# First attention layer of a two-layer decoder: token sums kept in the weight sum's tile, head 1's products in another order, rope ahead of the weight splits, the last head's keys turned later

## The chip, the cores and the metric

The kernel runs on one core of a Trainium2 chip. The time is the device time of one execution in microseconds (us), the median of several runs. TensorE (PE) does the matrix products and the transposes, PEld is its load of weights, VectorE is DVE, ScalarE is ACT, GpSimd is POOL and SyncE is SP. SP and POOL start most of the transfers.

## The reference

Two residual layers over 512 tokens of width 2048, all in float32: `x <- x + W_out(mixer(RMSNorm(x)) * silu(gate))`. The first mixer, which the change touches, is differential attention in 8 heads. The second is RWKV-7. Of the first:

```
proj = h @ w_in                                  # 2048 -> 4 x 2048
q, k, v, gate = jnp.split(proj, 4, axis=-1)      # 8 heads; q and k twice 128 wide, v and gate 256 wide
q = apply_rope(rms_norm(q, q_gain), cos, sin)
k = apply_rope(rms_norm(k, k_gain), cos, sin)
a = softmax(q0 k0') - lam * softmax(q1 k1')      # causal, scale 128 ** -0.5
o = rms_norm(a @ v, subln_w) * (1.0 - lambda_init)
return (o * silu(gate)) @ w_out
```

## The kernel before, in words

Float32 products are made of two halves: a value is split into a high part (a cast on ACT) and the rest (a subtraction on DVE), and `mm3` (L116) adds three matmuls: high by high, high by low, low by high. A weight tile of 128 by 512 is split by L618 (`wh`, ACT) and L619 (`wl`, DVE), each with four buffers; tokens of the normalised input lie split in `hH` and `hL`, 16 tiles of 128 channels by 512 tokens.

The first layer, some 800 us of the span, goes head by head. For a head, the queries and keys (512 columns) and the values and gates (512 columns) are one product of 512 tokens x 2048 channels x 1024 columns.

- *Head 0* uses two plain products, `unit_tok`: queries and keys first, then values and gates (PE from about 55 to 105 us). Its four PSUM banks hold 128 tokens each.
- *Heads 1 to 7* use Strassen's scheme in Winograd's form (`Seven`, L532): seven products P1 to P7, each half as wide in tokens (256), channels (1024) and columns, so 48 matmuls of 512 columns each. P1 to P5 and P7 need sums of tokens or of weights, or both; only P2 and P3 take weights and tokens as they lie. `Seven.T` (8 tiles of 128 x 512) holds the running weight sum: `prime` (L606) loads it for head 1, POOL adds further blocks to it by accumulating transfers (`grow`, L591), `renew` loads it for the next head. Two pairs of PSUM banks, A and B, take turns; `copy` and `take` (L640 to L648) move and add them on ACT and DVE.
- *The token sums* S1, S2 and S4 (`S`, each split into halves) and the tokens' difference that replaces a half of `hH` and `hL` are made once, in four groups, during the second product of head 0: `forms` and `form_sums`, L550 to L583. A group needs two scratch tiles of 2 x 512 columns, which before lie in the tiles (tags) of V, VL and G.
- *After the products* of a head, `queries` (L650) applies rope (`rope`, L298: squares for the norm on ACT, four products with the tables on DVE) and the norm (`norm_qk`, L318: a chain of small DVE operations, then L328 scales the keys on ACT), and `turn_qk` (L357) transposes queries and keys, block by block of 128 tokens, on PE (L361) and splits them (L364 on ACT, L365 on DVE) into `qkT` and `qkL`. `VG.convert` (L376) scales the values (V, VL), and makes the gate G (a tanh on ACT, L381, and its product with the raw gate on DVE, L382).
- *Attention* of a head runs during the products of the next one, cut into steps by a `Chain` (L124): after so many matmuls (`tick`) it takes its next step. The turning of keys is such a chain too: in heads 1 to 6 one block every 9 matmuls, 32 matmuls or more after the last product has been written; in the last head every 4, and what is left is finished as soon as the last product ends. The last head's attention lies within the first of the products with `da_w_out` (the out-projection), whose rows are read back from DRAM (`yd`) by `Feed` (L483), 14 rows of 256 KB in a ring of 8, half of them in the tiles `t1`.

Instructions are put in order by a scheduler with priorities: what stands under `high_priority` with the greater offset goes first on its engine: SCAN (5000) for the chains' steps, AHEAD (2000) for the weights' loads and splits, 0 for the forms. Each engine then runs its own list in order, so that an instruction that waits holds all behind it.

Head 1 begins with P3, P2, and its T is loaded during head 0. The others begin with P7, P2. The order in which the products end matters: P5's end gives the keys and queries, P3's or P5's the last values and gates.

Of the kernel before, what the change touches and what calls it, by code (L numbers as in the profile page):

```python
# [13 lines left out]
F32 = mybir.dt.float32  # L14
# [3 lines left out]
AF = mybir.ActivationFunctionType  # L18
# [5 lines left out]
P = 128  # L24
D = 2048
T = 512
KT = D // P
NT = T // P
NH = 8
# [9 lines left out]
AHEAD, SCAN, SOLVE = 2000, 5000, 4000  # L39
# [41 lines left out]
class Halves:  # L81


    def __init__(self, parts, n):
        self.parts, self.n = parts, n
# [209 lines left out]
        self.rr = g.small.tile([P, NT, 4], F32, name="rr", tag="rr", bufs=2)  # L295


def rope(g, q, t):  # L298

    nc, t1 = g.nc, q.t1s[t]  # L300
    t2 = g.work.tile([P, 512], F32, name="t2", tag="p1", bufs=1)
    for c in range(4):
        cs = slice(c * P, (c + 1) * P)
        nc.scalar.activation(t2[:, cs], t1[:, cs], AF.Square, scale=g.rstd0[:, t : t + 1],
                             accum_out=q.ss[:, t, c : c + 1])
    t1v = t1[:].rearrange("p (a b c) -> p a b c", a=2, b=2)
    t2v = t2[:].rearrange("p (a b c) -> p a b c", a=2, b=2)

    def tab(x, lo, hi):
        return x[:, t, :, None, lo:hi].to_broadcast([P, 2, 2, hi - lo])  # L310

    nc.vector.tensor_mul(t2v[:, :, :, 0:64], t1v[:, :, :, 64:128], tab(g.S, 0, 64))
    nc.vector.tensor_mul(t2v[:, :, :, 64:128], t1v[:, :, :, 0:64], tab(g.S, 64, 128))
    nc.vector.tensor_mul(t1v, t1v, tab(g.C, 0, P))
    nc.vector.tensor_add(t1[:], t1[:], t2[:])


def norm_qk(g, q):  # L318

    nc, ss, rr = g.nc, q.ss, q.rr  # L320
    nc.vector.tensor_scalar(ss[:], ss[:], 1.0 / P, EPS, ALU.mult, ALU.add)
    rsqrt(g, rr[:].rearrange("p t c -> p (t c)"), ss[:].rearrange("p t c -> p (t c)"), 4 * NT, "r16")
    nc.vector.tensor_mul(rr[:], rr[:], g.rstd0[:, :, None].to_broadcast([P, NT, 4]))
    nc.vector.tensor_scalar(q.sq[:], rr[:, :, 0:2], P ** -0.5, None, ALU.mult)
    for t in range(NT):
        for c in (2, 3):
            cs = slice(c * P, (c + 1) * P)
            nc.scalar.activation(q.t1s[t][:, cs], q.t1s[t][:, cs], AF.Copy, scale=rr[:, t, c : c + 1])  # L328


def head_qk(g, qk):

    q = QK(g)
    for t in range(NT):
        with g.tc.high_priority(offset=AHEAD):
            g.nc.scalar.copy(q.t1s[t][:], qk[t][:])
    for t in range(NT):
        rope(g, q, t)
    norm_qk(g, q)
    return q  # L340


def head_qkT(g):

    w = g.work
    return (w.tile([P, 4, T], F32R, name="qkT", tag="qkT", bufs=1),
            w.tile([P, 4, T], F32R, name="qkL", tag="qkL", bufs=1))


def keys(g, q, qkT, gap):  # L350

    for t in range(NT):
        turn_qk(g, q.t1s, *qkT, t)
        yield gap
# [128 lines left out]
class Feed:  # L483

    def __init__(self, g, src, n, home):
        self.g, self.src, self.n, self.home, self.raw, self.rows = g, src, n, home, [], []
        self.load(6)
        self.split(4)  # L490

# [8 lines left out]

    def __call__(self, n, m):
        self.split(n + 1, m)
        self.load(n + 8)


class Tokens:
# [25 lines left out]
class Seven:  # L532
# [11 lines left out]

    def banks(self):
        g = self.g
        self.B, self.A = [[g.pp.tile([P, 512], F32, name="pp", tag="pp") for _ in range(2)] for _ in range(2)]
        self.U, self.W = [[g.const.tile([P, 512], F32, name="u", tag=f"dd{i}{x}") for x in "HL"] for i in range(2)]

    def forms(self, n, _):  # L550

        i = self.made
        if i == len(GROUPS) or n < 4 * i + 5:
            return
        self.made += 1
        if i == 0:
            self.prime(1)
        with self.g.tc.high_priority(offset=0):
            self.form_sums(i)

    def form_sums(self, i):

        g, k0 = self.g, GROUPS[i][0]
        nc = g.nc
        f = lambda ap: ap.bitcast(F32)
        tops, lows = [g.work.tile([P, 2, 512], F32, name="form", tag=("V", "VL", "G", "qkL")[(2 * i + x) % 3], bufs=1)
                      for x in range(2)]
        for o, kb in ((tops, k0), (lows, KP + k0)):
            for k in range(2):
                nc.vector.tensor_add(o[:, k], f(g.hH[kb + k][:]), f(g.hL[kb + k][:]))  # L570
        (a, b), (c, d) = [(x[:, :, 0:256], x[:, :, 256:512]) for x in (tops, lows)]
        s1, s2, s4 = [[self.S[nm][i][:, :, x, :] for x in range(2)] for nm in ("S1", "S2", "S4")]
        for dest, o, x, y, op in ((s1, d, b, d, ALU.subtract), (None, b, a, b, ALU.subtract),
                                  (s2, a, d, a, ALU.subtract), (s4, c, c, a, ALU.add)):
            nc.vector.tensor_tensor(out=o, in0=x, in1=y, op=op)
            if dest:
                nc.scalar.copy(dest[0], o)
                nc.vector.tensor_sub(dest[1], o, f(dest[0]))
# [68 lines left out]
            for o, a, b in zip(out, x, y):  # L647
                self.g.nc.vector.tensor_tensor(out=o[:], in0=a[:], in1=b[:], op=op)  # L648

    def queries(self, q, last):  # L650

        for t in range(NT):
            rope(self.g, q, t)
        norm_qk(self.g, q)
        qkT = head_qkT(self.g)
        turning = Chain(self.g, keys(self.g, q, qkT, 4 if last else 9), 1, self.g.ticks + 32)
        self.turning = None if last else turning
        return qkT

    def head(self, h):  # L660
# [39 lines left out]
        def scores():  # L700
            self.take(q01, q01, A if h == 1 else B)
            self.take(q23, A if h == 1 else B, W, sub)
            q.t1s = q01 + q23
            return self.queries(q, h == NH - 1)

        if h == 1:
            q01.extend(q.more(2))
            self.product(B, *P3)
            self.product(A, *P2)
            self.copy(U, B)  # L710
            self.product(B, *P7)
            self.copy(W, A)
            self.take(U, U, A)
            self.product(A, *P1)
            self.copy(q01, B)
            self.take(q01, q01, W, sub)
            self.product(B, *P4)
            self.take(W, W, A)
            self.product(A, *P6)
            self.take(q01, q01, B, sub)  # L720
            self.take(W, W, B)
            self.product(B, *P5)
            qkT = scores()
            late = (W, B)
        else:
            self.product(B, *P7)
            self.product(A, *P2, end=False)
            q01.extend(q.more(2))
            self.copy(q01, B)
            self.product(B, *P1)  # L730
            self.copy(U, A)
            self.product(A, *P4, first=False)
            self.copy(W, B)
            self.product(B, *P6)
            self.take(q01, q01, A, sub)
            self.take(W, W, A)
            self.product(A, *P5)
            qkT = scores()
            self.product(B, *P3)
            self.take(W, W, A)  # L740
            late = (U, B)
        for c in [c for c in g.chains if c is not self.turning]:
            c.finish(g)
        vg = VG(g)
        self.take(late[0], *late)
# [152 lines left out]
def layer0(g, aps):  # L898
# [87 lines left out]
    with ExitStack() as cx:  # L986
        g.work = cx.enter_context(tc.tile_pool(name="work", bufs=2))
        u = Seven(g, aps)
        q, qkT = head_qk(g, qk0), head_qkT(g)
# [942 lines left out]
```

## Time and profile before

| | us |
|---|---|
| median of 3 runs | 2085.8 (2085.49 to 2088.36) |
| profiled execution | 2084.43 |
| its span | 2082.7 |
| granted clock of PE over the span | 0.996 |
| PE busy | 2054.2 |
| DVE busy | 1679.5 |
| ACT busy | 1280.3 |

All rows are of that one profiled execution. A row of the timeline has the start in us from the span's beginning, the duration in us, engine, line, operation, names out<-in, shape, and in brackets the idle time of the engine before it with what ended it. PE's durations overlap, so that its pace is read from the distance of starts. Where a name like `t` or `wh` is seen, the scratch number is left out. A row of the windows has the window, its length, the busy time and number of instructions of each engine, then PE's granted clock as a share of full speed, the share of time in which the transfer engines were busy, and GB/s.

### The profile page before, as it was taken

To read this page: it belongs to the slowest core of one execution; us is meant where nothing else is said; L and a number is where in the kernel's file an instruction comes from. 1 tells how busy PE (TensorE), PEld (TensorE's weight loads), DVE (VectorE), ACT (ScalarE), POOL (GpSimd) and SP (SyncE) were. 2 spreads that over 40 slices of the span, in tenths; PEclk is the share of its full clock that TensorE was granted. 3 is DMA by queue.
4 is the path that set the end of the run, shared out by engine and by line. 5 is a ranking of instruction groups with operands and counts; after the bars stand their busy time and mean duration, and the time that the engine had idled before them with its cause. 6 is when DMAs were issued, how large, how long until landed. Compare 5 with 4: busy or idle time off the path is not lost. (4 is left out here: it accounts for less than half of the span.)

```text
span 2082.7 us, 35269 instructions
## 1 busy us (share of the span) xinstructions
PE 2054.2 (99%) x11924; PEld 1693.2 (81%) x11924; DVE 1679.5 (81%) x4379; ACT 1280.3 (61%) x3043; POOL 419.9 (20%) x733
## 2 busy tenths in 40 slices
PE   9989999999999999999999999999999999999999
PEld 8868788888888878888778888888888888877887
DVE  5978797888878886576878888888888888887745
ACT  6666676767667664356666666666666666665433
POOL 0011201102121100101233222232332223232001
PEclk9999999999999999999999999999999999999999
DMA  6467867879687666752212222222222222244665
GB/s 201 144 123 167 168 169 159 182 168 173 173 175 176 139 219 211 180 124 94 84 64 79 71 87 76 86 79 79 71 85 77 73 82 79 79 121 159 218 162 121
DMA packets 100774, 269.71 MB, mean 130 GB/s; under 512 B 12432, under 2 KB 28960, under 8 KB 100592
## 3 DMA queue, kind: packets, MB, share of 16 engines
q1 hardware_dynamic: 62016, 173.21, 26.0%
q0 software_dynamic: 24144, 78.23, 20.7%
q10 hardware_dynamic: 14432, 16.01, 2.3%
q8 instruction: 94, 1.54, 0.3%
q14 instruction: 88, 0.72, 0.1%
HBM read 251.41 MB, written 15.99 MB: 128 GB/s over the span
## 5 line engine op out<-in xcount | busy, mean ns | idle before, releaser
L118 PE MATMUL pp<-hH,wh 128*128 128x512 f32 x1024 | 416.7, 407 | 0.0
L118 PE MATMUL pp<-hL,wh 128*128 128x512 f32 x1024 | 411.9, 402 | 0.0
L118 PE MATMUL pp<-hH,wl 128*128 128x512 f32 x1024 | 411.6, 402 | 0.0
L109 ACT CAST wh<-wraw 128x512 fp32r<-128x512 f32 (+1 forms) x412 | 254.2, 618 | 215.2 <-PE pp L118 122.8
L110 DVE TENSOR_TENSOR wl<-wraw,wh 128x512 fp32r<-128x512 f32 (+1 forms) x412 | 292.3, 711 | 76.5 <-ACT wh L109 70.9
L118 PE MATMUL pp<-wh,hH 128*128 128x512 f32 x820 | 325.5, 397 | 9.9 <-DVE G L382 8.2
L118 PE MATMUL pp<-wl,hH 128*128 128x512 f32 x820 | 324.4, 396 | 0.0
L118 PE MATMUL pp<-wh,hL 128*128 128x512 f32 x820 | 324.0, 396 | 0.0
L118 PEld LDWEIGHTS pp<-hH,wh 128*128 128x128 f32 x1024 | 192.8, 188 | 38.0 <-issue 2.1
L118 PEld LDWEIGHTS pp<-hH,wl 128*128 128x128 f32 x1024 | 193.1, 189 | 33.3
L118 PEld LDWEIGHTS pp<-hL,wh 128*128 128x128 f32 x1024 | 193.1, 189 | 31.3
L118 PE MATMUL pp<-wh,S 128*128 128x512 f32 x672 | 211.3, 391 | 0.0
L118 PEld LDWEIGHTS pp<-wh,hH 128*128 128x128 f32 x820 | 155.0, 189 | 41.3 <-issue 8.6
L618 ACT CAST wh<-T 128x512 fp32r<-128x512 f32 x224 | 137.3, 620 | 71.5 <-PE pp L118 52.3
L118 PEld LDWEIGHTS pp<-wh,hL 128*128 128x128 f32 x820 | 155.2, 189 | 30.4
L118 PEld LDWEIGHTS pp<-wl,hH 128*128 128x128 f32 x820 | 155.3, 189 | 30.0 <-DVE wl L619 0.3
L1631 POOL COPY SA<-VS 64x64 f32<-64x64 f32 x224 | 75.4, 337 | 516.3 <-DVE VS L1649 463.0
L619 DVE TENSOR_TENSOR wl<-T,wh 128x512 fp32r<-128x512 f32 x224 | 152.3, 688 | 20.5 <-ACT wh L618 18.5
L591 POOL DMA_DIRECT2D T<-in_da_w_in_dram x84 | 72.3, 861 | 396.6 <-DMA wraw<-in_da_w_in_dram 195.4
L118 PEld LDWEIGHTS pp<-wh,S 128*128 128x128 f32 x672 | 125.9, 188 | 25.7
L1496 DVE SCALAR_TENSOR_TENSOR tmpl<-LT,n,Tm 128x60 f32<-128x60 f32 (+24 forms) x496 | 135.6, 273 | 13.4
L118 PE MATMUL pp<-wl,S 128*128 128x512 f32 x336 | 131.8, 392 | 0.0
(376 smaller groups left out, 4019.8 us busy)
## 6 DMA issues: line engine op xcount, KB each, us to landing
wraw<-in_rw_w_in_dram SPq DMA_DIRECT2D x128, 512.0 KB, 3.7
T<-in_da_w_in_dram POOLq DMA_DIRECT2D x84, 512.0 KB, 5.8
wraw<-in_da_w_in_dram SPq DMA_DIRECT2D x64, 512.0 KB, 4.2
T<-in_da_w_in_dram SPq DMA_DIRECT2D x28, 512.0 KB, 4.0
wraw<-in_da_w_out_dram SPq DMA_DIRECT2D x26, 512.0 KB, 4.2
wraw<-in_rw_w_out_dram SPq DMA_DIRECT2D x26, 512.0 KB, 4.2
wraw<-in_da_w_in_dram POOLq DMA_DIRECT2D x21, 512.0 KB, 6.5
yr<-yd SPq DMA_DIRECT2D x20, 256.0 KB, 2.8
```

Of the source, the lines that this page charges most:

```text
L109: nc.scalar.copy(hi[:], raw[:, k : k + n])
L110: g.split = nc.vector.tensor_sub(lo[:], raw[:, k : k + n], hi[:].bitcast(F32)).ins
L118: m = nc.tensor.matmul(out, a, b, start=s, stop=e, skip_group_check=skip)
L591: self.g.nc.gpsimd.dma_start(out=raw, in_=src, accum_op=ALU.add)
L618: g.nc.scalar.copy(hi[:], raw[:, k])
L619: g.nc.vector.tensor_sub(lo[:], raw[:, k], hi[:].bitcast(F32))
L1496: st = nc.vector.scalar_tensor_tensor(tt, LT[:, i : i + 1, i + 1 :].to_broadcast([P, s, n]), n2[:, i : i + 1], Tm[:, 0:s, i : i + 1].to_br ...
L1631: nc.gpsimd.tensor_copy(p.SA[r_, c - 1, :], VS[r_, c, h, :])
```

## The change

- `rope` writes the squares' unused result into the new `qkL` (`junk`) and no longer into `t2`. The tiles `qkT` and `qkL` are therefore taken before rope.
- The token forms use slots 0 to 3 and 4 to 7 of T in turn. So T can be loaded for head 1 only when the forms are done: `prime(1)` moves from the first form to head 1, after P2.
- Head 1's order P3 P2 P7 P1 P4 P6 P5 becomes P2 P7 P1 P4 P6 P5 P3, with P2 unsummed, alone in its banks; its sums are made accordingly. Now in every head P3 comes last, after the sums of queries and keys (`take` of q01 and q23) and `queries`.
- Rope and norm of heads 1 to 7 stand at AHEAD, the priority of the weight splits. The turning starts 34 matmuls after (32 before), with 9 in between in the last head too, where it is no longer finished at the end of the last product.
- Head 0's converts stand at AHEAD.
- The out-projection's rows lie in slots 0 to 3, 6 and 7 of T, a ring of 6; the last attention's steps are 20 matmuls apart (22).

```diff
-def rope(g, q, t):
+def rope(g, q, t, junk):
...
-        nc.scalar.activation(t2[:, cs], t1[:, cs], AF.Square, scale=g.rstd0[:, t : t + 1],
+        nc.scalar.activation(junk[:, c, t * P : (t + 1) * P], t1[:, cs], AF.Square, scale=g.rstd0[:, t : t + 1],
                              accum_out=q.ss[:, t, c : c + 1])
...
     def __call__(self, n, m):
         self.split(n + 1, m)
-        self.load(n + 8)
+        self.load(n + self.ring)
...
         self.made += 1
-        if i == 0:
-            self.prime(1)
         with self.g.tc.high_priority(offset=0):
             self.form_sums(i)
...
-        tops, lows = [g.work.tile([P, 2, 512], F32, name="form", tag=("V", "VL", "G", "qkL")[(2 * i + x) % 3], bufs=1)
-                      for x in range(2)]
+        tops, lows = [self.T[:, k : k + 2] for k in (i % 2 * 4, i % 2 * 4 + 2)]
...
-    def queries(self, q, last):
-
-        for t in range(NT):
-            rope(self.g, q, t)
-        norm_qk(self.g, q)
+    def queries(self, q):
+
         qkT = head_qkT(self.g)
-        turning = Chain(self.g, keys(self.g, q, qkT, 4 if last else 9), 1, self.g.ticks + 32)
-        self.turning = None if last else turning
+        with self.ahead:
+            for t in range(NT):
+                rope(self.g, q, t, qkT[1])
+            norm_qk(self.g, q)
+        self.turning = Chain(self.g, keys(self.g, q, qkT, 9), 1, self.g.ticks + 34)
         return qkT
...
         if h == 1:
+            self.product(A, *P2)
+            self.prime(1)
+            self.product(B, *P7)
+            self.copy(U, A)
+            self.product(A, *P1)
             q01.extend(q.more(2))
-            self.product(B, *P3)
-            self.product(A, *P2)
-            self.copy(U, B)
-            self.product(B, *P7)
-            self.copy(W, A)
-            self.take(U, U, A)
-            self.product(A, *P1)
...
-            self.product(B, *P5)
-            qkT = scores()
-            late = (W, B)
+            A, B = B, A
         else:
...
-            self.product(A, *P5)
-            qkT = scores()
-            self.product(B, *P3)
-            self.take(W, W, A)
-            late = (U, B)
+        self.product(A, *P5)
+        self.take(q01, q01, B)
+        self.take(q23, B, W, sub)
+        q.t1s = q01 + q23
+        qkT = self.queries(q)
+        self.product(B, *P3)
+        self.take(W, W, A)
...
         out = VG(g)
-        for t in range(NT):
-            out.convert(g, t, vg[t])
+        with tc.high_priority(offset=AHEAD):
+            for t in range(NT):
+                out.convert(g, t, vg[t])
...
-        feed = Feed(g, g.yd, KT - 2, lambda k: g.work.tile([P, T], F32, name="yr", tag="t1", bufs=4)[:] if k & 4 else
-                    Tt[:, k % 4])
+        feed = Feed(g, g.yd, KT - 2, lambda k: Tt[:, (0, 1, 2, 3, 6, 7)[k % 6]], 6)
...
-        ch = Chain(g, attention(g, NH - 1, *before, 22, rows, Tt[:, 4:6]), 12)
+        ch = Chain(g, attention(g, NH - 1, *before, 20, rows, Tt[:, 4:6]), 12)
```

What this does to the order of the instructions is seen at three places (line numbers of the changed kernel are 3 lower around L560 to L650 and 10 lower from L1000 on).

First, DVE at the end of head 0. Before (S_709 is the last group's S1, S_713 its S2, S_717 its S4, `form` their scratch):

```order
L575 TENSOR_TENSOR form<-form 128x2x256 x2
L578 TENSOR_TENSOR S_709<-form,S_709 128x2x256
L619 TENSOR_TENSOR wl<-wraw,wh 128x512 x2
L583 TENSOR_TENSOR hL<-form,hH 128x256 x2
L575 TENSOR_TENSOR form<-form 128x2x256 x2
L578 TENSOR_TENSOR S_713<-form,S_713 128x2x256
L578 TENSOR_TENSOR S_717<-form,S_717 128x2x256
L379 SCALAR_TENSOR_TENSOR VL<-pp,rstd_595,V 128x256 x3
L382 SCALAR_TENSOR_TENSOR G<-G,pp 128x256 x3
L379 SCALAR_TENSOR_TENSOR VL<-pp,rstd_595,V 128x256
L382 SCALAR_TENSOR_TENSOR G<-G,pp 128x256
```

And after, where the scratch is T:

```order
L365 TENSOR_TENSOR qkL<-pt,qkT 128x4x128
L379 SCALAR_TENSOR_TENSOR VL<-pp,rstd_595,V 128x256
L572 TENSOR_TENSOR T<-T 128x2x256
L379 SCALAR_TENSOR_TENSOR VL<-pp,rstd_595,V 128x256
L382 SCALAR_TENSOR_TENSOR G<-G,pp 128x256
L575 TENSOR_TENSOR S_709<-T,S_709 128x2x256
L382 SCALAR_TENSOR_TENSOR G<-G,pp 128x256
L379 SCALAR_TENSOR_TENSOR VL<-pp,rstd_595,V 128x256
L616 TENSOR_TENSOR wl<-wraw,wh 128x512
L379 SCALAR_TENSOR_TENSOR VL<-pp,rstd_595,V 128x256
```

The converts (VL, G) stood behind the whole last group; now they stand beside its first difference. The rest of the group, S2 and S4, has moved some forty rows down, behind the layer's small constants and between head 1's first weight splits of T and the attention's first masks (L403):

```order
L572 TENSOR_TENSOR T<-T 128x2x256
L616 TENSOR_TENSOR wl<-T,wh 128x512
L580 TENSOR_TENSOR hL<-T,hH 128x256 x2
L572 TENSOR_TENSOR T<-T 128x2x256
L616 TENSOR_TENSOR wl<-T,wh 128x512
L572 TENSOR_TENSOR T<-T 128x2x256
L403 ISA sc,mx<-sc,mask 128x128
L403 ISA mx 128x1
L616 TENSOR_TENSOR wl<-T,wh 128x512
L406 SCALAR_TENSOR_TENSOR nb<-mx,sq 128x1
L403 ISA sc,mx<-sc,mask 128x128
L403 ISA mx 128x1
```

Right behind these rows stand the differences `S_713<-T,S_713`, one L406 and `S_717<-T,S_717`, with which the second half of T is free.

Second, SP around the load of T for head 1. Before (t_1483 and t_1484 are P2's last two weight tiles):

```order
L76 DMA wraw<-in_da_w_in_dram 128x1024 x6
L593 DMA T<-in_da_w_in_dram 128x1024 x4
L76 DMA wraw<-in_da_w_in_dram 128x1024 x4
L593 DMA wraw<-in_da_w_in_dram 128x1024 x3
L593 DMA t_1483<-in_da_w_in_dram 128x512
L593 DMA t_1484<-in_da_w_in_dram 128x512
```

And after, where those two tiles are t_1327 and t_1328:

```order
L76 DMA wraw<-in_da_w_in_dram 128x1024 x10
L590 DMA wraw<-in_da_w_in_dram 128x1024 x2
L590 DMA t_1327<-in_da_w_in_dram 128x512
L590 DMA t_1328<-in_da_w_in_dram 128x512
L590 DMA wraw<-in_da_w_in_dram 128x1024
L590 DMA T<-in_da_w_in_dram 128x1024 x4
```

The four loads of T stood ahead of the last loads of head 0; now they stand behind P2's.

Third, PE at the last head's keys. Before, behind 48 matmuls of the out-projection's first unit (t_7477 and t_7478 are blocks of 128 tokens of queries and keys, `sc` the scores of the last head's attention):

```order
L118 MATMUL pp<-wh,hL 128x512
L361 MATMUL pt<-ident,t_7477 128x128 x2
L118 MATMUL sc<-qkT 128x128 x2
L361 MATMUL pt<-ident,t_7478 128x128 x4
L118 MATMUL sc<-qkL,qkT 128x128
```

And after, behind 8 of them (the same two blocks are t_7469 and t_7470):

```order
L118 MATMUL pp<-wl,hH 128x512
L361 MATMUL pt<-ident,t_7469 128x128 x2
L118 MATMUL pp<-wh,hL 128x512
L118 MATMUL pp<-wh,hH 128x512
L118 MATMUL pp<-wl,hH 128x512
L118 MATMUL pp<-wh,hL 128x512 x2
L118 MATMUL pp<-wh,hH 128x512
L361 MATMUL pt<-ident,t_7470 128x128 x4
```

The blocks followed each other with the scores between them; now products of the unit lie between them.

More of the change, by code (lines that the diff above doesn't have):

```diff
@@ L328, in norm_qk, with head_qk @@
             nc.scalar.activation(q.t1s[t][:, cs], q.t1s[t][:, cs], AF.Copy, scale=rr[:, t, c : c + 1])
-def head_qk(g, qk):
+def head_qk(g, qk, junk):
     q = QK(g)
@@ L337, in head_qk @@
     for t in range(NT):
-        rope(g, q, t)
+        rope(g, q, t, junk)
     norm_qk(g, q)
@@ L483, with __init__ @@
 class Feed:
-    def __init__(self, g, src, n, home):
-        self.g, self.src, self.n, self.home, self.raw, self.rows = g, src, n, home, [], []
+    def __init__(self, g, src, n, home, ring=8):
+        self.g, self.src, self.n, self.home, self.ring, self.raw, self.rows = g, src, n, home, ring, [], []
         self.load(6)
@@ L546, in banks @@
         g = self.g
-        self.B, self.A = [[g.pp.tile([P, 512], F32, name="pp", tag="pp") for _ in range(2)] for _ in range(2)]
+        self.A, self.B = [[g.pp.tile([P, 512], F32, name="pp", tag="pp") for _ in range(2)] for _ in range(2)]
         self.U, self.W = [[g.const.tile([P, 512], F32, name="u", tag=f"dd{i}{x}") for x in "HL"] for i in range(2)]
@@ L698, in head @@
         sub = ALU.subtract
[L700 to L704, printed above, removed]
-        if h == 1:
+        if h == 1:
+            self.product(A, *P2)
[3 more added lines that the diff above has]
+            self.product(A, *P1)
             q01.extend(q.more(2))
-            self.product(B, *P3)
-            self.product(A, *P2)
-            self.copy(U, B)
-            self.product(B, *P7)
+            self.copy(q01, B)
+            self.take(q01, q01, U, sub)
+            self.product(B, *P4)
             self.copy(W, A)
-            self.take(U, U, A)
-            self.product(A, *P1)
-            self.copy(q01, B)
-            self.take(q01, q01, W, sub)
-            self.product(B, *P4)
-            self.take(W, W, A)
+            self.take(W, W, U)
             self.product(A, *P6)
@@ L736, in head @@
             self.take(W, W, A)
-            self.product(A, *P5)
-            qkT = scores()
-            self.product(B, *P3)
-            self.take(W, W, A)
-            late = (U, B)
+        self.product(A, *P5)
[5 more added lines that the diff above has]
+        self.take(W, W, A)
         for c in [c for c in g.chains if c is not self.turning]:
@@ L744, in head @@
         vg = VG(g)
-        self.take(late[0], *late)
+        self.take(U, U, B)
         with g.tc.high_priority(offset=AHEAD if h == NH - 1 else 0):
@@ L988, in layer0 @@
         u = Seven(g, aps)
-        q, qkT = head_qk(g, qk0), head_qkT(g)
+        qkT = head_qkT(g)
+        q = head_qk(g, qk0, qkT[1])
         Chain(g, keys(g, q, qkT, 20), 112)
```

## The prediction

> **What bounds the kernel now.** I read the page first: engines, then the waits of TensorE (PE) in the first 1200 us, which hold the first layer, then windows around the places where PE stood.
>
> ```profile
> span 2082.7 us, 35269 instructions
> PE 2054.2 (99%) x11924; PEld 1693.2 (81%) x11924; DVE 1679.5 (81%) x4379; ACT 1280.3 (61%) x3043; POOL 419.9 (20%) x733
> ...
> PE pp L118 <- DVE G L382: 8.2, 1, 8.2
> PE pt L361 <- ACT t L328: 2.9, 4, 1.6
> PE pt L361 <- issue: 2.3, 6, 1.1
> PE pp L118 <- ACT wh L618: 1.6, 1, 1.6
> PE pt L361 <- DVE qkL L365: 1.0, 2, 0.7
> PE sc L118 <- ACT qkT L364: 0.7, 1, 0.7
> ```
>
> PE is busy for 99% of the span, and the change neither adds nor takes away a product. So only PE's idle time and its slow time can be won. The rows (total, times, longest) list all of PE's idle time in the first layer that this change can touch: 8.2 us once for the gate G, and about 8.5 us around the turning of keys (L361 and what feeds it). The windows (length; busy time of PE, PEld, DVE, ACT, POOL; granted clock; DMA share; GB/s) show where, and that the clock falls there:
>
> ```profile
> 100.00:125.00 25.00, 16.82 (x69) 12.76 (x68) 19.26 (x54) 12.91 (x24) 0.00 (x0) 0.86 0.24 70
> 220.00:240.00 20.00, 17.18 (x79) 13.49 (x78) 12.21 (x34) 13.95 (x32) 4.96 (x6) 0.91 0.71 128
> 620.00:680.00 60.00, 59.81 (x286) 49.05 (x285) 51.28 (x127) 43.93 (x114) 9.46 (x11) 1.00 0.78 180
> 740.00:780.00 40.00, 36.36 (x171) 29.53 (x170) 33.19 (x114) 24.90 (x67) 1.34 (x2) 0.91 0.64 204
> 800.00:825.00 25.00, 25.00 (x112) 20.68 (x111) 12.81 (x22) 10.04 (x21) 2.83 (x4) 1.00 0.63 208
> ```
>
> Three places lose time: the end of head 0 (100 to 125), head 1's keys (220 to 240), the last head's keys (740 to 780). A head in between (620 to 680) loses 0.2 us in 60 at clock 1.00: nothing is to be had there, only to be lost. In the last row PE is full: 25.00 us over 112 products give 0.223 us each; I use 0.227, with the transposes' share.
>
> **End of head 0.** PE's rows (start, duration, what it waited for in brackets), then ACT's and DVE's:
>
> ```profile
> 104.77 0.39 PE L118 MATMUL pp<-wh,hL 128*128 128x512 f32 x1
> 113.34 0.77 PE L118 MATMUL pp<-wh,hH 128*128 128x512 f32 x1 [8.18 <-DVE G L382]
> ...
> 116.43 0.39 PE L118 MATMUL pp<-wl,hH 128*128 128x512 f32 x1
> 110.97 1.28 ACT L381 ACT_TABLE_LOAD   x1
> 108.66 1.42 DVE L578 TENSOR_TENSOR S<-form,S 128x512 fp32r<-128x512 f32 x2
> 110.19 1.27 DVE L379 SCALAR_TENSOR_TENSOR VL<-pp,rstd,V 128x256 fp32r<-128x256 f32 x3
> 112.78 1.15 DVE L382 SCALAR_TENSOR_TENSOR G<-G,pp 128x256 f32<-128x256 f32 x3 [1.31 <-ACT G L381]
> ```
>
> Head 1's first product needs PSUM banks that the converts of head 0's values and gates hold. These stood behind the last token forms on DVE (L578 ends at 110.1), because V, VL and G lay in the tiles of those forms. After the stall PE needs 116.43 - 113.34 = 3.09 us for seven matmuls, 1.59 at full speed: 1.5 us of slow clock. To be removed: 8.18 + 1.5 = 9.7 us.
>
> In the changed order the converts stand ahead of the last form's differences. V, the table load (1.28), G on ACT and G on DVE (1.15/3 = 0.38) then fit around PE's last matmuls, so I put G of the first bank at 104.5 to 105.3, a wait of **0.7 us** where 8.18 was.
>
> What the order gives back is the load of T. Head 1's summed product P7 reads T, but the forms now live there. Their last form stands behind the converts and behind the attention's first masks (L403):
>
> ```profile
> T<-in_da_w_in_dram SPq DMA_DIRECT2D x28, 512.0 KB, 4.0
> 126.82 0.29 DVE L403 CUSTOM_DVE_ANT_0 sc<-sc,mask 128x128 f32<-128x128 f32 x1
> 127.28 0.29 DVE L403 CUSTOM_DVE_ANT_0 sc<-sc,mask 128x128 f32<-128x128 f32 x1
> 716.70 0.68 DVE L648 TENSOR_TENSOR t<-t,pp 128x512 f32<-128x512 f32 x1
> 717.30 0.68 DVE L648 TENSOR_TENSOR t<-pp,u 128x512 f32<-128x512 f32 x1
> 224.79 0.62 ACT L618 CAST wh<-t 128x512 fp32r<-128x512 f32 x1 [0.33 <-DMA t<-in_da_w_in_dram]
> ```
>
> DVE starts a 512-wide operation every 0.60 us (717.30 - 716.70), a mask and its bias every 0.46. P2 starts near 105.4; a weight tile feeds six matmuls, 1.37 us. There are four buffers of split weights, so P7's first tile can be cast when P2's fifth is done, at 105.4 + 5 x 1.37 = 112.3; its wl follows at 112.9. From there the order holds three wl, three form differences, two hL halves, two masks and the differences of S2 and S4: 9 x 0.60 + 0.92 = 6.3 us; with some 0.6 us of standing for casts, T's second half is free near 119.8. The load takes 4.0 us, cast and wl 0.62 + 0.6 less the one matmul that does without wl: 124.7. PE, after P2 (48 x 0.227 = 10.9 us and 0.7 of small work), starts P7 at 117.0 and wants the fifth tile at 122.5 to 123: a wait of **2 us**, from 0 (the load in its window, DVE without a stand) to 4 (the load takes 2 us longer among the other transfers). I add 0.7 us for two late wl, since these rows now stand behind small constants, and 0.8 us of slow clock, between none and the 1.5 seen above. Sum: -9.7 + 0.7 + 2 + 0.7 + 0.8 = **-5.5 us**, from -9 to -3.
>
> At the clock, row and page are to be weighed. Small gaps beside ordinary matmuls did not lower it here (0.19 us, quoted below, in a window at 1.00); 8.18 us did. The Trainium skill, "TensorE: Matmul & The Clock Gate", section "Why this matters for your kernels", asks for "No PE-idle gaps >~3µs between matmul bursts": by it a lone wait of 2 us would cost no clock and the sum would be 0.8 us lower. Head 1's keys, next, fell to half speed with no single gap above 1.62 us; "Part 4: PE-mode transpose" of that page says that transposes do not count as busy in the same way, which would join those gaps to one of 3 us.
>
> **Head 1's keys.** Before, head 1 ended with P5 and its keys were turned while DVE was still at their norm:
>
> ```profile
> 221.11 0.33 PE L361 MATMUL pt<-ident,t 128*128 128x128 f32 x1 [0.50 <-ACT t L328]
> 223.19 0.66 PE L361 MATMUL pt<-ident,t 128*128 128x128 f32 x4 [0.70 <-DVE qkL L365]
> 225.46 1.12 PE L118 MATMUL pp<-wh,hH 128*128 128x512 f32 x2 [1.62 <-ACT wh L618]
> ```
>
> That is 0.50 + 0.70 + 1.62 = 2.8 us idle and 20 x (1 - 0.91) = 1.8 us of clock. Now a whole product, P3, lies between the keys' sums and their turning, as in heads 2 to 6. I take 4.6 away and leave 0.2: **-4.4 us**, bounds -5.4 (225.46 to 231 counted as half speed) and -2.
>
> **Heads 2 to 6.** The keys are now turned 32 matmuls (7.2 us) earlier, and rope and norm go ahead of the weight splits. What I compare is DVE's list with PE's arrival:
>
> ```profile
> 666.69 0.63 PE L361 MATMUL pt<-ident,t 128*128 128x128 f32 x4 [0.19 <-issue]
> 661.95 1.28 ACT L328 ACTIVATE t<-t,rr 128x128 f32<-128x128 f32 x4
> 628.00:654.50 26.50, 24.94 (x48) 1.00 0.66 182
> ```
>
> The sums start with P5 at 628.1. From there to the norms the new order has 26.2 us of DVE work: the last head's list, worked out below (25.3), and a split and a half for the next head (in before the same stretch was 24.94 of 26.50 us full), so they are ready at 654.3, L328's two halves 0.64 us each later, near 655.6. PE arrives after P5, P3 and 23 matmuls, 119 x 0.227 = 27.0 us: 655.1, plus the transposes of the queries: 655.6. Just in time; **0 us**, the cover being those 27 us. If it fails, each microsecond of lateness is paid five or six times: bounds -1 and +6 for all.
>
> **Last head.** Before, PE waited 1.57 + 0.72 + 0.29 + 1.05 = 3.6 us and ran at half speed from 755.68 to 761.52, 2.9 us more; 6.5 together.
>
> ```profile
> 751.51 0.62 PE L361 MATMUL pt<-ident,t 128*128 128x128 f32 x2 [1.57 <-ACT t L328]
> 752.85 0.44 PE L118 MATMUL sc<-qkT 128*128 128x128 f32 x2 [0.72 <-ACT qkT L364]
> 753.58 0.66 PE L361 MATMUL pt<-ident,t 128*128 128x128 f32 x4 [0.29 <-DVE qkL L365]
> 755.68 1.09 PE L361 MATMUL pt<-ident,t 128*128 128x128 f32 x4 [1.05 <-issue]
> ...
> 761.52 0.86 PE L118 MATMUL pp<-wh,hL 128*128 128x512 f32 x3
> 716.70:742.00 25.30, 24.08 (x47) 1.00 0.54 171
> ```
>
> Now the key columns stand behind only 8 matmuls of the out-projection, not 48, and turn one block at a time. PE arrives at 716.6 + 96 x 0.227 + 8 x 0.227 = 740.2, or 740.5 with transposes. DVE from 716.7 has 31 operations of 512 columns (18.6 us), 8 of 256 in rope (2.7), four converts (3.0) and the small norm chain (1.0): 25.3 us, 742.0 at best (the window shows it could fill such a stretch to 24.08 of 25.30). With L328 the keys are there at 743.1: a wait of **2.6 us**. Behind it DVE still owes two weight splits and the low half of the first yd row: 744.5, a second wait of **1.1 us**. With 1.7 us of slow clock that is 5.4 against 6.5: **-1.1 us**, from -6 (rope finishes early enough) to +2.
>
> **At nothing.** The Square's junk in qkL waits for the last scores of the head before, done half a head earlier. The row ring of six in T keeps five rows ahead, 13 us of PE work, over a load of 2.8 us:
>
> ```profile
> yr<-yd SPq DMA_DIRECT2D x20, 256.0 KB, 2.8
> ```
>
> Without that cover a row would cost those 2.8 us. On SP, T's load waits with P3's weights queued behind it; PE wants them five products, 54 us, later.
>
> **Sum.** -5.5 - 4.4 + 0 - 1.1 = -11 us. The profiled execution took 2084.4 us (2082.7 of span and 1.7 around it), so 2073.4; the median shown, 2085.8, lies 1.4 above it, so **2075 us**.
>
> **Rivals.** (a) *Little is given back*: DVE runs ahead of my lists, T lands in time, the last keys are ready. Then -9.0 - 4.6 - 6 = -19.6: 2066 us. For it: my DVE lists assume hardly any reordering; against: DVE was already full in both windows. (b) *More is given back*: T 4 us late with 1.5 us of clock, -2.8; head 1 at -2; last head +1: -3.8, 2082 us. (c) *Slower*: rope ahead of the splits starves PE at the keys of heads 1 to 6. The margin there is nil; if wl or attention's steps hold the norms 2 us more and the clock takes another 1.0, six turnings cost 18 us against 11: +7, 2093 us. It decides from 11/6 = 1.8 us a turning. Against it: 24.94 of 26.50 us full leaves some slack. (d) *No clock for short waits*: 0.19 us cost none and 8.18 us did; if a lone 2 us among ordinary matmuls falls on the first side, the wait for T loses its 0.8: 2074 us. The rule of the Trainium skill's page on TensorE and the clock gate, cited above, says so; the rows here leave it open. That the change does nothing at head 0 is excluded by the order of DVE.
>
> **How the numbers follow.** Forecast 0.50, (a) 0.25, (b) 0.13, (d) 0.06, (c) 0.06. The range reaches to (a) and (b) with a microsecond more on either side: 2065 to 2083. A measurement of this kernel tells about 0.2%, 4.2 us, from no change. Half of (b) falls within it: faster 0.50 + 0.25 + 0.06 + 0.06 = 0.87, same 0.08, slower 0.05.
>
> **What would show it.** PE's wait for G near 105 below 1 us; a wait near 123 for a cast of T; no wait and clock 1.00 near 220; heads 2 to 6 with waits below 0.3 us at the keys; two waits near 740 to 745. I am wrong if P7 never waits, if a head in between loses over 1 us, or if the last keys cost more than before.

## The result, and the profile after

The changed kernel takes 2072.9 us (median of 4 runs, 2072.6 to 2073.6), the kernel before 2085.6 beside it: ratio 0.9936, 95% interval 0.9919 to 0.9954. That is 12.7 us less; 2075 was forecast. The page's head and PE's waits in the first layer (total, times, longest) of the changed kernel:

```profile
span 2070.9 us, 35251 instructions
PE 2052.8 (99%) x11924; PEld 1692.9 (82%) x11924; DVE 1679.6 (81%) x4379; ACT 1278.5 (62%) x3043; POOL 420.6 (20%) x733
```

```profile
PE pt L361 <- ACT t L328: 2.6, 2, 2.0
...
PE pp L118 <- ACT wh L615: 1.4, 1, 1.4
...
PE pp L118 <- DVE hL L476: 0.7, 1, 0.7
...
PE pp L118 <- DVE G L382: 0.4, 2, 0.2
```

The wait for G has gone from 8.2 us to 0.4. In its place stands a wait for the cast of T (L615), and what is left of the waits at the keys stands in the last head. The windows after: two that were shown before, two long stages of the table below, and the two places where the clock fell:

```profile
100.00:125.00 25.00, 24.15 (x109) 18.57 (x107) 20.48 (x63) 15.41 (x32) 6.10 (x7) 1.00 0.76 145
220.00:240.00 20.00, 20.00 (x98) 16.76 (x97) 14.99 (x53) 13.82 (x32) 5.42 (x7) 1.00 1.01 180
240.00:720.00 480.00, 479.65 (x2304) 397.84 (x2304) 409.14 (x1120) 331.87 (x826) 75.49 (x88) 1.00 0.78 170
720.00:800.00 80.00, 76.71 (x359) 62.42 (x358) 62.90 (x184) 46.26 (x106) 2.97 (x4) 0.96 0.72 236
125.00:132.00 7.00, 5.83 (x20) 4.72 (x21) 3.90 (x11) 3.23 (x7) 1.57 (x2) 0.76 1.06 239
731.00:739.00 8.00, 6.82 (x19) 5.18 (x20) 5.59 (x11) 4.12 (x11) 0.00 (x0) 0.57 0.79 277
```

Before, the third and the fourth of these read:

```profile
240.00:720.00 480.00, 478.52 (x2305) 395.91 (x2304) 406.63 (x1143) 329.51 (x811) 76.84 (x90) 1.00 0.78 170
720.00:800.00 80.00, 75.99 (x353) 62.01 (x352) 67.28 (x195) 51.21 (x130) 1.58 (x3) 0.96 0.68 220
```

For a balance by stage I sum PE's excess in each profile: the distance between the starts of neighbouring matmuls, less 0.2265 us for 512 columns and in proportion for fewer. It holds the waits, the slow clock, and a steady share of transposes. (It is worked out from the starts in the traces; no row shows it.)

| kernel | 80 to 160 us: G, T | 160 to 240: head 1's keys | 240 to 720: heads 2 to 6 | 720 to 800: last head |
|---|---|---|---|---|
| before | 14.1 | 7.7 | 20.8 | 11.5 |
| after | 9.2 | 2.9 | 18.6 | 10.3 |
| difference | -4.9 | -4.7 | -2.2 | -1.2 |
| forecast | -5.5 | -4.4 | 0 | -1.1 |

The four sum to -13.0; before 80 us and after 800 us 1.2 us more is seen, without a wait of its own. The part after 800 us lies between 111.2 and 112.2 us in kernels that hardly differ there, so that a difference of 1 us in one profile can be scatter.

Two waits are given back. The first is the load of T. DVE's last form, SP's load of T's second half (two transfers), ACT's cast of it and PE's waits, all after:

```profile
119.92 0.69 DVE L575 TENSOR_TENSOR S<-T,S 128x512 fp32r<-128x512 f32 x1
...
120.00 0.95 SPq L590 DMA_DIRECT2D T<-in_da_w_in_dram  x2
...
125.27 1.14 ACT L615 CAST wh<-T 128x512 fp32r<-128x512 f32 x2 [3.69 <-DMA T<-in_da_w_in_dram]
...
125.94 0.49 PE L118 MATMUL pp<-wh,S 128*128 128x512 f32 x1 [1.43 <-ACT wh L615]
126.66 0.50 PE L118 MATMUL pp<-wl,S 128*128 128x512 f32 x1 [0.23 <-DVE wl L616]
```

SP starts the load at 120.0, as the sum had it (119.8); the first transfer takes 5.2 us, not 4.0; PE wants it at 124.5, not 122.5 to 123. The wait is 1.43 + 0.23 us, and the clock then falls (0.76 in the window above, 1.7 us in 7).

The second is at the last head's keys. The end of the norm on DVE, then PE, after:

```profile
730.84 0.18 DVE L323 TENSOR_TENSOR rr<-rr,rstd 128x16 f32<-128x16 f32 x1
...
731.50 0.77 PE L361 MATMUL pt<-ident,t 128*128 128x128 f32 x2 [2.04 <-ACT t L328]
732.95 0.79 PE L118 MATMUL pp<-wh,hL 128*128 128x512 f32 x1 [0.68 <-DVE hL L476]
```

These are the two waits foreseen, 2.0 and 0.7 us (2.6 and 1.1 were the forecast). The clock behind them is 0.57 over 8 us, 3.4 us of slow clock where 1.7 was forecast.

### The profile page after: what moved, and what is told of

The parts are those of the page before. It is cut to its first block, busy times and chain, and to the rows that moved or that the text cites. A ratio compares the mean times of both kernels' runs of the same rounds, so it can differ in the third digit from the quotient of the medians.

```text
span 2070.9 us, 35251 instructions
## 1 busy us (share of the span) xinstructions
PE 2052.8 (99%) x11924; PEld 1692.9 (82%) x11924; DVE 1679.6 (81%) x4379; ACT 1278.5 (62%) x3043; POOL 420.6 (20%) x733
## 3 DMA queue, kind: packets, MB, share of 16 engines
q8 instruction: 94, 1.54, 0.3%
## 5 line engine op out<-in xcount | busy, mean ns | idle before, releaser
L118 PE MATMUL pp<-wh,S 128*128 128x512 f32 x672 | 216.4, 396 | 1.4 <-ACT wh L615 1.4
L615 ACT CAST wh<-T 128x512 fp32r<-128x512 f32 x224 | 138.1, 620 | 110.9 <-PE pp L118 96.4
```

What stands on the lines that cost most here:

```text
L118: m = nc.tensor.matmul(out, a, b, start=s, stop=e, skip_group_check=skip)
L615: g.nc.scalar.copy(hi[:], raw[:, k])
```

## The experiments

All times are medians, with the kernel before run beside them (2085.6 to 2086.3 us). The excess is of the one profiled run, by the stages of the table above; it moves with what that run's clock did (last section).

| run | us | ratio to before, 95% | excess by stage |
|---|---|---|---|
| E1 before, converts ahead | 2086.4 | 1.0000 (0.9991 to 1.0009) | 14.5, 7.6, 20.7, 11.9 |
| E2 after, converts not ahead | 2074.5 | 0.9946 (0.9931 to 0.9961) | 11.1, 3.2, 18.9, 11.0 |
| E3 before, head 1 in the new order | 2081.4 | 0.9978 (0.9969 to 0.9987) | 14.2, 3.3, 20.6, 10.9 |
| E4 after, rope not ahead | 2070.9 | 0.9924 (0.9908 to 0.9941) | 11.1, 3.7, 21.0, 6.1 |
| E5 after, constants later | 2067.9 | 0.9914 (0.9900 to 0.9927) | 5.0, 3.8, 18.7, 7.8 |
| E6 after, rope not ahead in the last head | 2065.9 | 0.9903 (0.9887 to 0.9918) | 8.4, 3.0, 18.6, 5.6 |
| E7 after, last keys later still | 2073.2 | 0.9937 (0.9925 to 0.9950) | 9.4, 2.9, 18.6, 12.3 |
| E8 E5 and E6 | 2064.4 | 0.9895 (0.9881 to 0.9908) | 6.7, 3.8, 18.6, 5.5 |
| E9 E6, turning as before | 2069.3 | 0.9920 (0.9905 to 0.9935) | 9.7, 3.2, 18.6, 7.0 |
| E10 E9, rows in t1 as before | 2070.9 | 0.9926 (0.9909 to 0.9942) | 9.4, 2.9, 18.7, 8.8 |
| E11 before, rows in T | 2083.5 | 0.9987 (0.9978 to 0.9996) | 14.9, 7.6, 21.3, 9.3 |
| E12 E11, squares into qkL | 2080.2 | 0.9969 (0.9957 to 0.9981) | 15.5, 7.1, 20.7, 6.9 |

**The end of head 0: tiles or priority (E1, E2).** E1 gives the kernel before the converts' priority alone:

```diff
-        for t in range(NT):
-            out.convert(g, t, vg[t])
+        with tc.high_priority(offset=AHEAD):
+            for t in range(NT):
+                out.convert(g, t, vg[t])
```

> The kernel before, with only head 0's converts put at the splits' priority. Theory: the priority alone does nothing, because V, VL and G still lie in the tiles of the token forms and have to wait for the last of them; the order of DVE around them is the same as before. So PE waits 8.2 us for G again and the time is that of before, 2085.6 us within 1. Rival: the low priority of the converts was what cost; then the wait falls below 2 us and the time is about 2077.

```profile
114.15 0.77 PE L118 MATMUL pp<-wh,hH 128*128 128x512 f32 x1 [8.19 <-DVE G L382]
```

The wait is the old one to 0.01 us, and the time is unchanged: the priority alone does nothing. E2 takes the same lines back out of the changed kernel, so that it has the tiles alone.

> The changed kernel, with head 0's converts back at the default priority; the forms stay in T. Theory: the tiles make the converts free, the priority puts them ahead. Without it the last forms' rows stand ahead of G on DVE again: G of the first bank near 108.7 instead of 105.1, so PE waits about 3.8 us there, some 0.9 at the second bank, and the clock takes 1.5; in return the forms are done near 109.5, T is loaded in time, and the wait for it (1.7 us and its slow clock, 3.3 together) is gone. Sum +2.9: 2075.8 us. Rival (tiles alone do it, the priority is idle): 2072.9. Rival (the wait for T has another cause than the late forms): it stays, 2079.

```profile
109.73 0.76 PE L118 MATMUL pp<-wh,hH 128*128 128x512 f32 x1 [4.58 <-DVE G L382]
```

PE waits 4.6 us for G (3.8 + 0.9 expected, in one piece), and no wait for the cast of T is left, since the forms are done first. The net is +1.7 us (2.9 expected), with the wait for the load gone in return. So the tiles make the converts free, and only then does the priority work; and the late forms are what T waits for.

**Head 1's keys (E3).** The kernel before with head 1 in the order P2 P7 P1 P4 P6 P5 P3, all else as it was:

```diff
-            self.product(B, *P3)
-            self.product(A, *P2)
-            self.copy(U, B)
-            self.product(B, *P7)
...
+            self.product(A, *P2)
+            self.product(B, *P7)
+            self.copy(U, A)
+            self.product(A, *P1)
```

> The kernel before, with only head 1's order changed to P2 P7 P1 P4 P6 P5 P3 and its sums with it; forms in the old tiles, T loaded early, rope at the default priority, last keys as before. Theory: a product now lies between the keys' sums and their turning, so head 1's 2.8 us of waits and the slow clock behind them go, 4.4 us as in the changed kernel; the 8.2 us for G and the last head stay. 2081.2 us. Rival (rope's priority is what removed head 1's waits): less than 1.5 us is won, 2084 or more.

2081.4 us, 4.4 us less, as expected; the excess of its stage falls from 7.7 to 3.3. Of the three waits at head 1's keys one short one is left, which stands in heads 2 to 6 of this run too:

```profile
218.97 0.63 PE L361 MATMUL pt<-ident,t 128*128 128x128 f32 x4 [0.18 <-issue]
```

The order alone did it; rope's priority had no part there.

**Rope's priority (E4, E6, E7).** E4 takes it away in all heads, E6 in the last alone. The lines are E6's; E4 drops the `with`:

```diff
-        with self.ahead:
+        with self.g.tc.high_priority(offset=0) if last else self.ahead:
             for t in range(NT):
                 rope(self.g, q, t, qkT[1])
```

> The changed kernel, with rope and norm of heads 1 to 7 back at the default priority. In this order the norm of a head stands some 2.5 us of DVE work later and the key blocks on PE are written some 8 matmuls (1.8 us) later. Theory (the just-in-time reading of heads 2 to 6): the late place covers most of it, heads 1 to 6 lose 0 to 1 us each, the last head 1 us more: +1 to +7, 2076 us. Rival (rope's priority does nothing anywhere): 2072.9 within 0.7. Rival (without it PE starves at every turning, 2.5 us and the clock): +18, 2091 us.

> The changed kernel, with rope and norm at the default priority in the last head alone. The order then puts the last keys behind some 52 matmuls of the out-projection, not 8, with the products at the splits' pace until then. Theory, from the run with rope low in all heads (0.5 us of waits there and clock 1.00): the last head's 2.0 + 0.7 us of waits and the slow clock go, 4.2 us; heads 1 to 6 keep their 0.07 us. 2068.7 us. Rival (what was won in that run lay elsewhere): 2072.9 within 1.

E4 was expected to lose and won 2 us (its four runs lie between 2068.7 and 2072.3). In heads 1 to 6 it lost what the theory said: 0.44 us of waiting at each turning, 21.0 against 18.6 of excess in heads 2 to 6. Its profiled run also waited 2.95 us for T, at a place that the edit does not touch. But in the last head it won 4.2: PE meets the first key block behind 53 products of the unit, not 8, and waits 0.5 us where it had waited 2.7.

```profile
211.81 0.66 PE L361 MATMUL pt<-ident,t 128*128 128x128 f32 x4 [0.44 <-DVE qkL L365]
...
745.06 0.33 PE L361 MATMUL pt<-ident,t 128*128 128x128 f32 x1 [0.54 <-ACT t L328]
```

E6 keeps what was won in the last head and drops the loss elsewhere: 2065.9 us (2068.7 expected), the last head at 5.6, with its windows' row now

```profile
720.00:800.00 80.00, 78.90 (x380) 64.05 (x379) 63.99 (x186) 46.48 (x108) 2.96 (x4) 1.00 0.73 237
```

so PE idles 1.1 us there, not 3.3, at full clock. Of its 7.0 us against the changed kernel 4.7 are the last head's; in its profiled run the waits for T were also shorter, two of 0.7 and 0.8 us without a slower clock, at a place that the edit does not touch. E7 tries the same end by the step's place in the program, with rope still ahead:

```diff
-        self.turning = Chain(self.g, keys(self.g, q, qkT, 9), 1, self.g.ticks + 34)
+        self.turning = Chain(self.g, keys(self.g, q, qkT, 9), 1, self.g.ticks + 34 + later)
```

with `later` 30 in the last head, its attention 4 matmuls behind and its steps 18 apart.

> The changed kernel, rope ahead, with the last head's turning 30 matmuls later in the program (64 after, not 34), its attention 4 matmuls behind that (12) and its steps 18 apart (20). On PE the first key block then stands about 9 matmuls, 2.0 us, later and the scores 30 later. Theory (only the place of the keys is wrong): the wait of 2.04 us falls below 0.3, that for the row's low half below 0.5, the clock stays up, 3.5 to 4 us are won: 2069.1 us; the row halves may take 0.5 back. Rival (DVE is what is full there, the debt moves along): waits of over 1.5 us stay behind the keys or at the rows, 2072 or more.

```profile
733.51 0.50 PE L118 MATMUL pp<-wh,hL 128*128 128x512 f32 x1 [3.72 <-DVE hL L476]
```

The theory fell, the rival held: 2073.2 us, the wait at the keys is gone, and PE stands 3.7 us for the low half of a row instead. DVE still does rope before the unit's splits, so PE only meets DVE's late work at another place. What helps, by E6, is the other order on DVE: the splits first and the keys after.

**The load of T (E5, E8).** The constants and, behind them, the first head's attention begin 40 matmuls later:

```diff
         g.chains[0].step(g)
+        g.chains[0].wait = 50
         u.banks()
```

> The changed kernel, with the second layer's small constants, and with them the first head's attention behind, begun 40 matmuls later (after 50 of head 1's instead of 10). The 21 small rows and the masks then stand behind the last forms on DVE. Theory (T is late because its forms are): the second half of T is free some 3.4 us earlier, loaded before PE wants it, and the wait of 1.4 + 0.2 us with its slow clock, 3.3 us in all, goes: 2069.6 us. Rival (the load itself is slow among the other transfers, the forms are not what it waits for): the wait stays, 2072.9 within 1.

```profile
115.81 0.69 DVE L575 TENSOR_TENSOR S<-T,S 128x512 fp32r<-128x512 f32 x1
```

The last form is done 4.1 us earlier, and PE has no wait for T. 2067.9 us, 5.0 less where 3.3 was expected; the excess of the stage falls by 4.2. At head 1's keys 0.9 comes back, with a wait of 0.52 us for `qkL`; in the last head, which the edit does not touch, 2.5 more goes, since the clock stayed up there in this profile (last section). E8 has this and E6's edit.

> The changed kernel with both: constants 40 matmuls later, and rope and norm low in the last head. Theory (two separate waits at two places): the gains add, 3.3 + 4.2: 2065.4 us. Rival (the first gain is given back later, as PE arrives earlier at the keys): 2068 or more.

2064.4 us (2065.4 expected): both places are cured at once, and it is the fastest kernel here, 21.8 us under the one before. Its two windows:

```profile
80.00:160.00 80.00, 78.58 (x359) 62.51 (x358) 67.98 (x184) 48.04 (x102) 14.61 (x17) 1.00 0.79 168
720.00:800.00 80.00, 78.90 (x380) 64.08 (x379) 64.19 (x186) 46.47 (x108) 2.96 (x4) 1.00 0.72 235
```

**What freed the last keys (E9 to E12).** E9 is E6 with the last turning written as before (a block every 4 matmuls, the rest at the product's end; the start stays at 34, the attention's steps at 20), E10 also with the rows' old home and ring:

```diff
-        self.turning = Chain(self.g, keys(self.g, q, qkT, 9), 1, self.g.ticks + 34)
+        turning = Chain(self.g, keys(self.g, q, qkT, 4 if last else 9), 1, self.g.ticks + 34)
+        self.turning = None if last else turning
```

```diff
-        feed = Feed(g, g.yd, KT - 2, lambda k: Tt[:, (0, 1, 2, 3, 6, 7)[k % 6]], 6)
+        feed = Feed(g, g.yd, KT - 2, lambda k: g.work.tile([P, T], F32, name="yr", tag="t1", bufs=4)[:] if k & 4 else
+                    Tt[:, k % 4], 8)
```

> The run with rope low in the last head, with that head's turning again written as in the kernel before: a block every 4 matmuls, what is left finished at the end of P3. On PE the blocks then stand where they stood without it, since their place follows from when the norm is ready and not from where the step is written. Theory (the step's place in the program is idle, what freed the last keys is that rows and keys no longer share tiles): 2066 us within 1. Rival (the later turning, which the change is named after, is what won there): back to 3 us of waits and the slow clock, 2071 us.

> The same, and the out-projection's rows as before: half of them in the tiles t1, which the last queries and keys hold until they are transposed, a ring of 8. Theory (this sharing is why PE stood at the last keys before: the unit has no fifth row until a block is turned, so that there is nothing to put between the blocks): the waits at the keys come back, some 3 us of them, and with them the clock's 2: 2071 us. Rival (the rows' home costs nothing, as the prediction had it): 2066 us within 1.

E9's keys stand where E6's do on PE (behind 53 products) and its last head costs 7.0 against 5.6, of which 0.8 is a wait for the unit's last rows: the later turning is worth some 1.4 us, not nothing and not five. In time E9 is 3.4 us above E6, more than that: its profiled run also waited 2.2 us for T, with 3.4 us at half speed behind. E10 adds 1.9 in the last head. Neither theory nor rival is met in full: the keys wait little, but PE stands for a row that had no tile. Its load into t1 starts at 738.1, when the first block has been turned, and lands at 742.0:

```profile
742.66 0.50 PE L118 MATMUL pp<-wh,hH 128*128 128x512 f32 x1 [2.14 <-ACT hH L475]
```

Since E10 still was 2.7 better than before in the last head, E11 put the rows into T, with the ring of six, in the kernel before, and E12 the squares into qkL as well (the same lines as in the change).

> The kernel before, with only the out-projection's rows changed: all in slots 0 to 3, 6 and 7 of T, a ring of 6. On PE the first key block then stands behind 66 products of the unit, not 48, and products lie between the blocks. Theory (rows and last keys sharing the tiles t1 is what made PE stand at the last keys): the 3.6 us of waits there fall below 1, the clock stays up, 5.5 us of the last head's 6.5 are won: 2080.2 us. Rival (it needs the later turning or the other edits as well): less than 2 us is won, 2084 or more.

```profile
793.08 0.41 PE L446 MATMUL yt<-ident,G 128*128 128x128 f32 x2 [1.39 <-DVE G L441]
794.71 0.79 PE L118 MATMUL pp<-wh,hH 128*128 128x512 f32 x1 [1.22 <-ACT hH L475]
```

In the last head all waits at the keys but one of 0.26 us are gone, as the theory had it; but the keys now come so late (66 products) that the last rows, which hang on the last head's attention, are late at the unit's end: 2.6 us and the clock given back. 2.2 us of 5.5 are won (2.3 in time).

> The kernel before, with the out-projection's rows in T as in the run with the rows alone, and besides the squares' unused result in qkL (in head 0 too). In the order the first key block moves from behind 66 products of the unit to behind 53, the last transposed attention from behind 168 to 166; the row that hangs on it is the unit's product 168. Theory (squares and rope took turns in the tile t2, the next block's squares waiting for DVE's sum, which made the norm late): the waits of 1.4 + 1.2 us and the slow clock at the unit's end shrink to about 0.8 us, some 2.3 us are won: 2081.2 us. Rival (the squares' tile costs nothing, as the prediction had it): 2083.5 us within 0.7.

2080.2 us, 2081.2 expected. In the kernel before, ACT's squares waited for DVE's rope, block after block, since both used one tile; with the result in qkL they do not. A row of the kernel before:

```profile
743.27 0.40 ACT L304 ACTIVATE t<-t,rstd 128x128 f32<-128x128 f32 x1 [1.93 <-DVE t L315]
```

The last square starts at 731.8 in E12, at 745.5 before. The keys stand behind 53 products, the row waits 0.8 us, and the last head costs 6.9.

So the last head's -1.2 is a sum of large parts: rows in T -2.2 (11.5 to 9.3), squares in qkL -2.4 (to 6.9), the later turning -1.4 (E9 to E6), rope ahead +4.7 (5.6 to 10.3); between E12 and E9, where the closer steps come in, 0.1 is left. These sizes hold for these profiles: half or more of the first, second and last is slow clock (6.8 us at half speed in the last head before and after, 3.4 in E11, none in E12, E9 and E6). With rope ahead and the clock up, in E5, the last head cost 7.8, so that rope ahead takes 2.2 by its waits and up to 4.7 with the clock.

## Why the prediction was right, and where it was not

- **The end of head 0.** The wait for G was forecast at 0.7 us and is 0.4. The wait for T came as argued, by the chain argued: forms behind constants and masks, SP's load at 120.0, shown by E2 and E5, which end the wait from two sides. Three of its terms were off and partly cancelled, which is luck: the load took 5.2 us instead of 4.0, PE came 1.5 us later, and the slow clock was 1.7 us instead of 0.8. The load is the loosest term. In six kernels with the same order at this place (after, E4, E6, E7, E9, E10) it took 4.4 us (E6) to 6.7 (E4), and PE waited 0.7 to 2.95 us for it, the longer the longer it took; the median of 4.0 that the sum used lies below all of them, and why is not shown. -5.5 forecast, -4.9 measured.
- **Head 1's keys.** -4.4 forecast, -4.7 in the stage, and -4.4 by E3 alone.
- **Heads 2 to 6.** Forecast 0, measured -2.2. The comparison of DVE's list with PE's arrival held: PE idles 0.07 us a head. The failed step is the base, "nothing is to be had there": I compared arrival with readiness and left out the waits that were there to be removed. PE's idle time in the window fell from 1.48 to 0.35 us; the rest lies in matmuls that start closer to each other, at a granted clock of 1.00 before and after. E3 and E4, without rope's priority, stay at 20.6 and 21.0: it is that priority which brings the 2.2.
- **The last head.** The two waits came as foreseen, somewhat shorter, with twice the slow clock. That the number agrees as well (-1.1 against -1.2) is luck, because "At nothing" was wrong twice: the rows' home and the squares' tile are worth 2.2 and 2.4 us. I had looked for what they cost, and found cover; they were what held the last keys. Nor did I see the price of rope's priority there, 2.2 to 4.7 us: it makes the norm early enough that the order puts the keys behind 8 products, and makes the splits late that those products need.
- **The rivals.** (a), little given back, did not occur, but E8 shows that it was there to be had: 2064.4 us against its 2066, with the 2.2 of heads 2 to 6 in it. (b), more given back, is refuted by the time, 10 us under its 2082. (c), rope starving PE in heads 1 to 6, is refuted by E4: there its absence costs. (d), no slow clock behind a lone short wait, is refuted for the changed kernel: the granted clock behind 1.43 + 0.23 us was 0.76 over 7 us. That goes against the rule that the prediction cites from the Trainium skill ("TensorE: Matmul & The Clock Gate", "Why this matters for your kernels"), and the measurement decides; that it is not so each time stands below.

## What to carry to other kernels

When a tile is shared by two steps, look for who is held by it, not only whether its new home costs something: two such edits, thought free, were worth 4.6 us of the last head's excess here, slow clock included. Rope's priority helped in heads 2 to 6, where DVE had slack (busy for 409 of 480 us), and cost time in the last head, where DVE was full (3.41 of 3.41 us before the slow clock, next section): try a priority by stage, and let the last stage, which has other work, have its own. And when readiness is compared with arrival, subtract what is waited for today.

## What the runs showed of the hardware

Whether a wait of 1.5 to 3 us costs PE's clock differs from run to run. In E5's profile the last keys waited as long as in the changed kernel, and the clock stayed up:

```profile
728.10 0.62 PE L361 MATMUL pt<-ident,t 128*128 128x128 f32 x2 [2.15 <-ACT t L328]
729.55 0.50 PE L118 MATMUL pp<-wh,hL 128*128 128x512 f32 x1 [0.82 <-DVE hL L476]
```

```profile
725.00:735.00 10.00, 7.02 (x35) 5.18 (x34) 9.19 (x24) 7.07 (x18) 0.00 (x0) 1.00 0.77 270
```

The record of the granted clock in the traces shows a pattern. In all 14 profiles the clock changes only on a grid of 3.41 us, whose start in the span differs from profile to profile (6 to 9 us), and while the kernel runs a slow stretch is at half speed for one, two or three steps (3.4, 6.8 or 10.2 us). The step before the changed kernel's second slow stretch and that stretch, then E5's two steps at the same waits:

```profile
728.25:731.66 3.41, 1.37 (x7) 0.81 (x5) 3.41 (x15) 2.28 (x8) 0.00 (x0) 1.00 0.68 225
731.66:738.49 6.83, 6.15 (x17) 4.65 (x17) 4.74 (x9) 3.51 (x10) 0.00 (x0) 0.50 0.80 277
724.08:727.49 3.41, 1.87 (x9) 1.21 (x7) 3.41 (x13) 2.23 (x5) 0.00 (x0) 1.00 0.66 227
727.49:730.90 3.41, 1.97 (x8) 1.41 (x9) 3.41 (x9) 2.93 (x9) 0.00 (x0) 1.00 0.63 209
```

In the changed kernel PE idled 2.04 us of one step; in E5 the longer wait fell across a border, and PE idled 1.54 and 1.44 us of two. I counted so through all whole steps at full clock of the 14 profiles, idle being the step less PE's busy time: of the 17 in which PE idled 1.95 us or more, each was followed by half speed; of the 8374 with less than 1.3 us none was; of the 11 between, six were. This is read from the traces; no run moved a wait against the grid on purpose.

The four runs of E5 took 2066.2 and 2066.4 us at a mean clock of 1.000, 2069.4 at 0.999 and 2071.7 at 0.998: the spread of 5.5 us goes with the clock. E6 and E8, whose profiles hold no wait of over 0.8 us in these stages, show a clock of 1.000 in every run, and theirs lie within 1.3 and 2.3 us. A wait of about 2 us therefore has a price of itself, or of itself and 1.7 us more for each step at half speed (one or two steps here), and a single run does not tell which.
